# Loads and stores of H, of the filter blocks, of the bias table and of the heads' scales issued from GpSimd's queue, in a two-layer attention and long-convolution encoder on one Trainium2 core

## The chip, the core and the metric

The kernel runs on one core of one Trainium2 chip. The metric is the device time of one execution in microseconds (us), launch to end. Before the change three runs gave 963.81, 966.33 and 965.6 us, with a median of 965.6 us. The engines are called as the profile does: PE (matmul), PEld (its weight loads), DVE (vector), ACT (scalar), POOL (GpSimd), SP (the engine that here only issues transfers). "SPq" is SP's own sequence of transfer issues, "POOLq" that of POOL.

## The reference, cut to what matters

```python
DEPTH, SEQ, D_MODEL = 2, 512, 1024
for l in range(DEPTH):
    h = rms_norm(x, pre_norm[l], NORM_EPS)
    q, k, v, z_a, u_h, z_h, g_a, g_h = jnp.split(h @ w_in[l], splits, axis=-1)
    o = diff_attention(q, k, v, lam, rel_bias)             # 4 heads, two softmaxes each, table of relative biases
    o = rms_norm(o, subln[l], SUBLN_EPS) * (1.0 - lam_init)
    y_a = o * jax.nn.silu(z_a)
    hv, hx1, hx2 = jnp.split(short_conv3(u_h, conv_w[l], conv_b[l]), 3, axis=-1)
    filt = hyena_filters(S, ..., flt_w_out[l], flt_deltas[l])   # rfft of long filters, made from small weights
    z = fft_long_conv(hv, filt[:, 0], flt_bias[l, 0]) * hx1
    z = fft_long_conv(z, filt[:, 1], flt_bias[l, 1]) * hx2
    m = jax.nn.sigmoid(g_a) * (y_a @ w_pa[l]) + jax.nn.sigmoid(g_h) * (z * jax.nn.silu(z_h)) @ w_ph[l]
    x = x + rms_norm(m @ w_out[l], post_norm[l], NORM_EPS)
```

## The kernel before, in words

All work is in float32, and every product is made of three matmuls on operands split in two: `split` lets ACT cast the source to `hi` (line 207) and DVE form `lo = source - hi` (line 208). Weights come in blocks of 256 KB: `weights` loads a block into `wraw` (three buffers), and splits it into `whi` and `wlo`. The buffer of a block is free when DVE has made its `wlo`.

The stages of a layer follow one another, but are mixed: the norm of four row tiles of 128 (`ss`, `rinm` on DVE at line 224, `rin` on POOL at line 226, the scaling `s` on DVE at line 519, transposes on PE at line 530, `hT`), then the input projection; four attention heads (`head_rows`, `head_norm`, `head_scale`); the long convolutions, done as matrix products with blocks of a Fourier matrix (`fh`, `fl`, constants that POOL fetches at the start); the output projections; and the border to the next layer (`routm` and `rout`, then again `rinm` and `rin`).

The filters of the convolutions don't depend on x. They are computed in eight blocks for the layers' two orders and two channel halves, in gaps of the other stages: `filter_load` fetches `flt_deltas`, `flt_w_out` (in two pieces) and `flt_bias`; `filter_group` makes a piece of the spectrum and stores it to a tensor in DRAM, `H` (`H_408` to `H_411`). The convolutions read it back into `ld` (two buffers) and `hb` (one). A head loads its bias rows from the table `tab`, which the kernel has written to DRAM, into `ld`. `head_norm` makes the scale of a head's rows on POOL (`ro`, line 689); `head_scale` transposes it on PE (line 696), writes 2 KB to DRAM (`rd`), reads it back spread over all partitions (`b`, three buffers), and DVE multiplies with it (line 703).

No order is written out by hand beyond this. A list scheduler with costs and priorities of its own (`high_priority`, `ahead`) places every instruction in its engine's sequence, and each engine then works through its sequence in order: an issue that waits for a buffer holds all that stands behind it on the same engine. Before the change SP issues every transfer (`load` at line 181, `store` at line 184) but four, which POOL issues: `fh` and `fl` (line 252), `a3d` (line 361) and `a` from `a3d` (line 407).

Of the kernel before, what the change touches and what calls it, by code (L numbers as in the profile page):

```python
# [17 lines left out]
P = 128  # L18
# [116 lines left out]
def ahead(n):  # L135

    def wrap(f):
        def g(self, *args):
            with self.tc.high_priority(offset=n):
                return f(self, *args)  # L140
        return g
    return wrap
# [3 lines left out]
class Net:  # L146
# [35 lines left out]

    def store(self, out, src):
        self.nc.sync.dma_start(out=out, in_=src)

    def mm3(self, out, pairs):

        n = 3 * len(pairs)
        i = 0
        for lh, ll, rh, rl in pairs:  # L190
            for l, r in ((lh, rh), (lh, rl), (ll, rh)):
                self.nc.tensor.matmul(out, lhsT=l, rhs=r, start=(i == 0), stop=(i == n - 1))  # L192
                i += 1
# [209 lines left out]
    def filter_load(self, l, o, hc, st):  # L403
        nc, a = self.nc, self.a
        if l and o == hc == 0:
            self.a3 = self.cst.tile([P, 512], F32R, name="a3", tag="a3")
            nc.gpsimd.dma_start(out=self.a3, in_=self.a3_next)
        raw = self.t("b", a=2)
        dl = self.t("yh", a=4)[:, 0:2] if st["where"] == "convs" else self.t("u", a=2)
        self.load(dl, a["flt_deltas"][l].rearrange("(d o h c) -> d o h c", d=2, o=2, h=2)[:, o, hc].partition_broadcast(P))  # L410
        src = a["flt_w_out"][l].rearrange("k (d o h c) -> k d o h c", d=2, o=2, h=2)[:, :, o, hc]
        for j in range(2):
            self.load(raw[j * 64:(j + 1) * 64], src)
        nc.scalar.activation(out=dl, in_=dl, func=AF.Abs)
        hi, lo = (self.t("u" if st["where"] == "heads" else "za", F32R, 2) for _ in range(2))
        self.split(hi, lo, raw)
        st.update(dl=dl, hi=hi, lo=lo, T=[self.two(st) for _ in range(2)])
        br = st["bias"] = self.sm.tile([P, 256], F32, name="fbias", tag="fbias", bufs=1)
        self.load(br[0:1, :], a["flt_bias"][l, o:o + 1, hc * 256:hc * 256 + 256])

    @ahead(-20)
    def filter_taps(self, l, t, st):
# [49 lines left out]
    def filter_group(self, l, o, hc, im, ft, st):  # L472

        nc = self.nc
        ps = self.ps("po", 2)
        yh, yl = st["in", im, ft ^ im]
        f, c = "EO"[ft], "CS"[im]
        even = [(c + "E" + f, yh[:, 0], yl[:, 0])]
        if im == 0:
            zh, zl = st["in", 0, 0]  # L480
            even.append((("FA", "FB")[ft], zh[:, 0], zl[:, 0]))
        self.dft_sum(ps[:, 0], even)
        self.dft_sum(ps[:, 1], [(c + "O" + f, yh[:, 1], yl[:, 1])])

        s = 1.0 * 2 / NF if ft else self.nt[:, NT_RE + im:NT_RE + im + 1]
        odd, hs = self.t("b", a=2)[:, 0], self.t("b", a=2)
        nc.scalar.activation(out=odd, in_=ps[:, 1], func=AF.Copy, scale=s)
        for j, op in ((0, ALU.add), (1, ALU.subtract)):  # L490
            nc.vector.scalar_tensor_tensor(out=hs[:, j], in0=ps[:, 0], scalar=s, in1=odd, op0=ALU.mult, op1=op)
        H = self.H[l][o][:, hc]
        if ft:
            self.store(H[:, 6 + 2 * im:8 + 2 * im], hs)
        elif im:
            self.store(H[:, 4:6], hs)
            d = self.t("b", a=2)
            for j in range(2):
                nc.scalar.activation(out=d[0:1, j], in_=ps[0:1, 1], func=AF.Copy, scale=(1.0 - 2 * j) / NF)
            self.store(H[0:1, 1:4:2], d[0:1])  # L500
        else:
            self.store(H[:, 0:4:2], hs)
            self.store(H[:, 1:4:2], hs)


    def new_hT(self):
# [115 lines left out]
    @ahead(20)  # L622
    def head_rows(self, l, h, i, st):


        nc = self.nc
        if i == 0:
            st["B"] = self.t("ld")
            t = self.tab[h:h + 1, :]
            self.load(st["B"][:, :896], bass.AP(tensor=t.tensor, offset=t.offset + 1, ap=[[1, P], [1, 896]]))  # L630
            st["s"] = self.small(8, "s")
        tsl = slice(i * P, (i + 1) * P)
        s0, s1 = (st["s"][:, 4 * c + i:4 * c + i + 1] for c in range(2))
        p = []
        for c in range(2):
            ps = self.ps("pq")
            for n in range(2):
                nc.tensor.matmul(ps, lhsT=st["q"][c][:, tsl], rhs=st["k"][c][n], start=(n == 0), stop=(n == 1))  # L638
            lg = self.t("a")
            m = self.small(1, f"m{c}")  # L640
            nc.vector.tensor_tensor_reduce(out=lg, in0=ps, in1=st["B"][:, 384 - i * P:896 - i * P], scale=1.0, scalar=3e38,  # L641
                                           op0=ALU.add, op1=ALU.min, accum_out=m)
            nc.scalar.activation(out=lg, in_=lg, func=AF.Exp, scale=-1.0, bias=m, accum_out=(s0, s1)[c])  # L643
            p.append(lg)
        r = self.small(1, "r")
        nc.vector.reciprocal(out=r, in_=s1)
        n1 = self.small(1, "n1")
        nc.vector.scalar_tensor_tensor(out=n1, in0=r, scalar=self.nlam[:, l:l + 1], in1=s0, op0=ALU.mult, op1=ALU.mult)
        nc.vector.scalar_tensor_tensor(out=p[0], in0=p[1], scalar=n1, in1=p[0], op0=ALU.mult, op1=ALU.add)
        st[i] = p[0]  # L650
# [41 lines left out]
    def head_scale(self, l, h, st):  # L692
        nc = self.nc
        u, pss, r = st["u"], st["o"], st["r"]

        nc.tensor.transpose(out=pss[0:4, 128:256], in_=r, identity=self.ident)
        rows = self.t("b")
        nc.scalar.copy(out=rows[0:4, :P], in_=pss[0:4, 128:256])
        rd = self.dram.tile([4, P], F32, name=f"rd{l}{h}", tag=f"rd{l}{h}")
        self.store(rd, rows[0:4, :P])  # L700
        rb = self.t("b")
        self.load(rb, rd.rearrange("i q -> (i q)").partition_broadcast(P))
        nc.vector.tensor_tensor(out=tiles(u), in0=tiles(u), in1=tiles(rb)[:, :, ::-1], op=ALU.mult)
        hi, lo = self.t("ya", F32R), self.t("ya", F32R)
        self.split(hi, lo, u)
        self.ya.append((hi, lo))
# [87 lines left out]
    @ahead(30)  # L794
    def conv_group(self, l, o, hc, st, ft):

        nc = self.nc
        H = self.H[l][o][:, hc]
        first, b = self.t("ld", a=4), None
        if ft:  # L800
            self.load(first, H[:, 6:10])
            A, B = first[:, 0:2], first[:, 2:4]
        else:
            B = self.t("hb", a=2)
            self.load(first, H[:, 0:4])
            self.load(B, H[:, 4:6])
        yh, yl = st["Y"]
        f = "EO"[ft]
        U = [self.ps("pq", 2) for _ in range(2)]
        for j, t in enumerate("EO"):  # L810
            re = [("C" + t + f, yh[:, j], yl[:, j])]
            im = [("S" + t + f, yh[:, 2 + j], yl[:, 2 + j])]
            if t == f == "E":
                re.append(("XA", yh[:, 2], yl[:, 2]))
                im.append(("XB", yh[:, 0], yl[:, 0]))
            self.dft_sum(U[j][:, 0], re)
            self.dft_sum(U[j][:, 1], im)
        odd = self.t("a", a=2)
        nc.scalar.copy(out=odd, in_=U[1])

        X, W = self.t("cx", a=4), self.t("cx", a=4)
        for s, op in ((0, ALU.add), (1, ALU.subtract)):
            nc.vector.tensor_tensor(out=X[:, 2 * s:2 * s + 2], in0=U[0], in1=odd, op=op)  # L823
        four = lambda t: t.rearrange("p (s c) x -> p s c x", s=2)
        both = lambda t: t.rearrange("p (s c) x -> p s c x", c=1).broadcast_to([P, 2, 2, 256])
        nc.vector.tensor_tensor(out=four(W), in0=four(X), in1=both(B), op=ALU.mult)  # L826
        nc.vector.tensor_tensor(out=four(X), in0=four(X), in1=both(A) if ft else four(first), op=ALU.mult)  # L827
        nc.vector.tensor_tensor(out=X[:, 0:4:2], in0=X[:, 0:4:2], in1=W[:, 1:4:2], op=ALU.subtract)
        nc.vector.tensor_tensor(out=X[:, 1:4:2], in0=X[:, 1:4:2], in1=W[:, 0:4:2], op=ALU.add)

        for s, op in ((0, ALU.add), (1, ALU.subtract)):
            nc.vector.tensor_tensor(out=W[:, 2 * s:2 * s + 2], in0=X[:, 0:2], in1=X[:, 2:4], op=op)  # L832
        st["Q", f] = self.t("s1", F32R, 4), self.t("s1", F32R, 4)
        self.split(*st["Q", f], W)
# [264 lines left out]
```

## Time and profile before

| what | value |
|---|---|
| runs | 963.81, 966.33, 965.6 us; median 965.6 |
| profiled execution | 964.57 us, of which the span is 962.8 |
| PE busy | 920.7 us (96%) |
| DVE busy | 734.0 us (76%) |
| ACT busy | 467.6 us (49%) |
| POOL busy | 42.0 us (4%) |
| mean granted TensorE clock | 0.993 |

The span runs from the first to the last instruction of the profiled execution; 1.77 us of its time lie around it. An engine's busy time doesn't count the issuing of transfers; that is seen in the timelines of SPq and POOLq, where a row's first number is the start of an issue and its second its duration. In a timeline, the bracket at the end of a row gives the idle time ahead of it on its engine and what ended it.

### The profile page before, as it was taken

What the parts mean: (1) busy time and instruction counts of PE and PEld (TensorE: products, weight loads), DVE (VectorE), ACT (ScalarE), POOL (GpSimd) and SP (SyncE); (2) the same over time, 40 slices, a digit from 0 to 9 for tenths busy, and PEclk for the clock granted to TensorE, in tenths of its full rate; (3) what the DMA queues carried; (4) which work ended last, traced back from release to release, by engine and by line L of the source; (5) the groups of instructions that cost most, each with busy time, mean ns of one, the idle gap of its engine ahead of it and who ended that gap; (6) DMA issues with size and microseconds to landing.
All of it is one profiled execution on the core that took longest, in us unless ns stands there. A gap on an engine that the chain in (4) does not pass through costs nothing. (4 is left out here: it accounts for less than half of the span.)

```text
span 962.8 us, 14325 instructions
## 1 busy us (share of the span) xinstructions
PE 920.7 (96%) x5139; PEld 793.0 (82%) x5139; DVE 734.0 (76%) x1439; ACT 467.6 (49%) x927; POOL 42.0 (4%) x58
## 2 busy tenths in 40 slices
PE   3999999999899989999999999999999998999997
PEld 3878988887788878878889888888888887888897
DVE  4889789789889978888657486686798898854533
ACT  4586576555344334555435465564444433333431
POOL 2000100002000000000001000000000000000000
PEclk9999999999999999999999999999999999999999
DMA  7341541533534443345645323333343644233422
GB/s 243 108 135 53 151 131 51 166 104 87 148 115 128 123 114 117 102 129 153 208 133 165 92 85 96 88 89 117 91 121 88 197 121 125 82 90 98 139 71 88
DMA packets 147692, 114.18 MB, mean 119 GB/s; under 512 B 7106, under 2 KB 134752, under 8 KB 147621
## 3 DMA queue, kind: packets, MB, share of 16 engines
q1 hardware_dynamic: 147045, 111.31, 39.1%
q0 software_dynamic: 576, 1.97, 0.6%
q8 instruction: 40, 0.66, 0.3%
q14 instruction: 31, 0.25, 0.1%
HBM read 98.26 MB, written 14.99 MB: 118 GB/s over the span
## 5 line engine op out<-in xcount | busy, mean ns | idle before, releaser
L192 PE MATMUL pd<-hT,whi 128*128 128x512 f32 x1408 | 455.1, 396 | 3.1 <-ACT a L887 2.6
L192 PEld LDWEIGHTS pd<-hT,whi 128*128 128x128 f32 x1408 | 261.0, 188 | 55.3 <-ACT a L887 3.3
L192 PE MATMUL pd<-hT,wlo 128*128 128x512 f32 x704 | 278.2, 395 | 3.7 <-DVE wlo L208 3.6
L207 ACT CAST whi<-wraw 128x512 fp32r<-128x512 f32 x228 | 140.9, 619 | 222.1 <-PE pd L192 112.8
L208 DVE TENSOR_TENSOR wlo<-wraw,whi 128x512 fp32r<-128x512 f32 x228 | 154.6, 686 | 67.4 <-ACT whi L207 66.5
L192 PEld LDWEIGHTS pd<-hT,wlo 128*128 128x128 f32 x704 | 132.5, 188 | 30.9 <-DVE wlo L208 4.5
L643 ACT ACTIVATE a<-a,m 128x512 f32<-128x512 f32 x64 | 46.1, 721 | 21.8 <-DVE m L641 20.7
L638 PE MATMUL pq<-s,s 128*128 128x512 f32 x128 | 47.1, 402 | 1.4 <-DVE m L641 1.3
L641 DVE CUSTOM_DVE_ANT_0 a<-pq,ld 128x512 f32<-128x512 f32 x64 | 43.1, 685 | 3.8 <-PE pq L638 3.1
L192 PE MATMUL pd<-whi,hT 128*128 128x256 f32 x192 | 38.8, 298 | 5.6 <-ACT whi L207 5.6
L722 DVE SCALAR_TENSOR_TENSOR u<-pd,vec,u 128x256 f32<-128x256 f32 (+2 forms) x80 | 39.3, 530 | 3.6 <-ACT u L720 3.3
L192 PE MATMUL pd<-ya,whi 128*128 128x512 f32 x128 | 41.7, 393 | 0.0
L192 PE MATMUL pd<-yh,whi 128*128 128x512 f32 x128 | 39.5, 389 | 0.0
L192 PEld LDWEIGHTS pd<-whi,hT 128*128 128x128 f32 x192 | 32.2, 202 | 6.3 <-ACT whi L207 6.2
L204 PE MATMUL po<-s,fh 128*128 128x256 f32 x160 | 31.4, 296 | 4.6 <-ACT s L207 2.0
L207 ACT CAST s<-cx 128x1024 fp32r<-128x1024 f32 x24 | 25.2, 1050 | 21.9 <-DVE cx L832 19.0
L204 PE MATMUL pq<-s,fh 128*128 128x256 f32 x160 | 34.7, 291 | 0.0
L204 PEld LDWEIGHTS po<-s,fh 128*128 128x128 f32 x160 | 26.0, 199 | 7.3 <-ACT s L207 2.8
L935 DVE TENSOR_TENSOR yh<-pd,s 128x256 f32<-128x256 f32 x32 | 13.3, 421 | 24.0 <-ACT a L933 23.3
L208 DVE TENSOR_TENSOR s<-cx,s 128x1024 fp32r<-128x1024 f32 x24 | 29.3, 1222 | 0.8 <-ACT s L207 0.8
L638 PEld LDWEIGHTS pq<-s,s 128*128 128x128 f32 x128 | 23.2, 188 | 7.7 <-DVE m L641 2.5
L192 PE MATMUL po<-s,yh 128*128 128x256 f32 x192 | 28.8, 285 | 0.5 <-ACT s L207 0.4
(221 smaller groups left out, 1661.5 us busy)
## 6 DMA issues: line engine op xcount, KB each, us to landing
wraw<-in_w_in SPq DMA_DIRECT2D x192, 256.0 KB
H<-b SPq DMA_DIRECT2D x40, 256.0 KB
ld<-H SPq DMA_DIRECT2D x16, 512.0 KB
wraw<-in_w_out SPq DMA_DIRECT2D x32, 256.0 KB
wraw<-in_w_pa SPq DMA_DIRECT2D x16, 256.0 KB
wraw<-in_w_ph SPq DMA_DIRECT2D x16, 256.0 KB
ld<-tab SPq DMA_DIRECT2D x8, 448.0 KB
yh<-in_x SPq DMA_DIRECT2D x4, 512.0 KB
```

What stands on the lines that cost most here:

```text
L192: self.nc.tensor.matmul(out, lhsT=l, rhs=r, start=(i == 0), stop=(i == n - 1))
L204: self.nc.tensor.matmul(out, lhsT=b, rhs=y, start=(i == 0), stop=(i == len(ops) - 1))
L207: self.nc.scalar.copy(out=hi, in_=src)
L208: self.nc.vector.tensor_tensor(out=lo, in0=src, in1=hi.bitcast(F32), op=ALU.subtract)
L638: nc.tensor.matmul(ps, lhsT=st["q"][c][:, tsl], rhs=st["k"][c][n], start=(n == 0), stop=(n == 1))
L641: nc.vector.tensor_tensor_reduce(out=lg, in0=ps, in1=st["B"][:, 384 - i * P:896 - i * P], scale=1.0, scalar=3e38, op0=ALU.add, op1=ALU.min ...
L643: nc.scalar.activation(out=lg, in_=lg, func=AF.Exp, scale=-1.0, bias=m, accum_out=(s0, s1)[c])
L722: nc.vector.scalar_tensor_tensor(out=o, in0=src, scalar=w[j], in1=o, op0=ALU.mult, op1=ALU.add)
L935: nc.vector.tensor_tensor(out=st["o"][tt][:, cs], in0=ps, in1=g, op=ALU.mult)
```

## The change

A new helper `side` issues a transfer from POOL's queue. 128 transfers, until then issued by SP, go through it: for each of the eight filter blocks one load of `flt_deltas`, two of `flt_w_out` and one of `flt_bias` (32); 48 stores to H (40 of 256 KB, 8 of 2 KB); 8 loads of 448 KB from `tab`; 8 stores of 2 KB to `rd` and 8 loads of 256 KB from it; 24 loads of H (16 of 512 KB into `ld`, 8 of 256 KB into `hb`). The weights, x, the gains, the constants, and the stores of x and of the output stay with SP.

```diff
+    def side(self, out, src):
+
+        self.nc.gpsimd.dma_start(out=out, in_=src)
+
@@ filter_load
-        self.load(dl, a["flt_deltas"][l].rearrange("(d o h c) -> d o h c", d=2, o=2, h=2)[:, o, hc].partition_broadcast(P))
+        self.side(dl, a["flt_deltas"][l].rearrange("(d o h c) -> d o h c", d=2, o=2, h=2)[:, o, hc].partition_broadcast(P))
...
-            self.load(raw[j * 64:(j + 1) * 64], src)
+            self.side(raw[j * 64:(j + 1) * 64], src)
...
-        self.load(br[0:1, :], a["flt_bias"][l, o:o + 1, hc * 256:hc * 256 + 256])
+        self.side(br[0:1, :], a["flt_bias"][l, o:o + 1, hc * 256:hc * 256 + 256])
@@ filter_group
-            self.store(H[:, 6 + 2 * im:8 + 2 * im], hs)
+            self.side(H[:, 6 + 2 * im:8 + 2 * im], hs)
...
@@ head_rows
-            self.load(st["B"][:, :896], bass.AP(tensor=t.tensor, offset=t.offset + 1, ap=[[1, P], [1, 896]]))
+            self.side(st["B"][:, :896], bass.AP(tensor=t.tensor, offset=t.offset + 1, ap=[[1, P], [1, 896]]))
@@ head_scale
-        self.store(rd, rows[0:4, :P])
+        self.side(rd, rows[0:4, :P])
         rb = self.t("b")
-        self.load(rb, rd.rearrange("i q -> (i q)").partition_broadcast(P))
+        self.side(rb, rd.rearrange("i q -> (i q)").partition_broadcast(P))
...
-            self.load(first, H[:, 0:4])
-            self.load(B, H[:, 4:6])
+            self.side(first, H[:, 0:4])
+            self.side(B, H[:, 4:6])
```

The other stores and loads of H are edited in the same way. The scheduler plans anew with these issues on POOL, so the sequences of the other engines change at places too; of PE's 5,104 instructions the first 146 rows of its sequence stand as before, then some groups are exchanged. Line numbers of the changed kernel are 4 higher behind the helper, and the moved transfers have the helper's line, 188.

On DVE the start of the program reads so before the change. `s_141` to `s_302` are the four row tiles of x on their way to `hT`, `wlo` the lower halves of the first weight blocks.

```order
L224 TENSOR_SCALAR rinm<-ss 128x1
L519 SCALAR_TENSOR_TENSOR s_141<-yh,rin,s_127 128x512 x2
L224 TENSOR_SCALAR rinm<-ss 128x1
L519 SCALAR_TENSOR_TENSOR s_192<-yh,rin,s_127 128x512 x2
L208 TENSOR_TENSOR hT<-pt,hT 128x2x128
L224 TENSOR_SCALAR rinm<-ss 128x1 x2
L519 SCALAR_TENSOR_TENSOR s_248<-yh,rin,s_127 128x512
L208 TENSOR_TENSOR wlo<-wraw,whi 128x512 x3
L208 TENSOR_TENSOR hT<-pt,hT 128x2x128 x2
L519 SCALAR_TENSOR_TENSOR s_248<-yh,rin,s_127 128x512
L208 TENSOR_TENSOR hT<-pt,hT 128x2x128 x2
L208 TENSOR_TENSOR wlo<-wraw,whi 128x512
```

The same piece of DVE's sequence after the change:

```order
L228 TENSOR_SCALAR rinm<-ss 128x1 x2
L523 SCALAR_TENSOR_TENSOR s_141<-yh,rin,s_127 128x512 x2
L523 SCALAR_TENSOR_TENSOR s_192<-yh,rin,s_127 128x512 x2
L228 TENSOR_SCALAR rinm<-ss 128x1
L523 SCALAR_TENSOR_TENSOR s_248<-yh,rin,s_127 128x512
L212 TENSOR_TENSOR wlo<-wraw,whi 128x512
L212 TENSOR_TENSOR hT<-pt,hT 128x2x128
L212 TENSOR_TENSOR wlo<-wraw,whi 128x512 x2
L212 TENSOR_TENSOR hT<-pt,hT 128x2x128 x2
...
L212 TENSOR_TENSOR wlo<-wraw,whi 128x512
L212 TENSOR_TENSOR hT<-pt,hT 128x2x128 x2
L228 TENSOR_SCALAR rinm<-ss 128x1
```

The `rinm` of the second row tile now stands ahead of `s_141`, and that of the fourth behind the fourth `wlo`. POOL's `rin` of a tile needs that tile's `rinm`, and `fh` and `fl` stand behind all four `rin` in POOL's sequence in both kernels.

On POOL the border of the layers and the first two heads of layer 1 read so before (`s_5936` to `s_6824` are parts of the heads' keys that are set to zero):

```order
L226 TENSOR_TENSOR rout<-routm,nhalf 128x1
L226 TENSOR_TENSOR rin<-rinm,nhalf 128x1
L611 MEMSET s_5936 64x512
L611 MEMSET s_5941 64x512
...
L689 TENSOR_TENSOR ro<-rom,nhalf 128x4
L611 MEMSET s_6819 64x512
L611 MEMSET s_6824 64x512
L689 TENSOR_TENSOR ro<-rom,nhalf 128x4 x3
```

And after the change, the same stretch of POOL from the last `rout` of the border to the second `ro` of layer 1 (the rows left out are a `rin`, MEMSETs and two more `ld<-tab`):

```order
L188 DMA ld<-tab 128x896
L230 TENSOR_TENSOR rout<-routm,nhalf 128x1
...
L188 DMA ld<-tab 128x896
L693 TENSOR_TENSOR ro<-rom,nhalf 128x4
L188 DMA rd_6492<-b 4x128
L188 DMA b<-rd_6492 128x512
L615 MEMSET s_6819 64x512
L188 DMA yh<-in_flt_deltas 128x2x256
L615 MEMSET s_6824 64x512
L188 DMA ld<-H_410 128x1024
L693 TENSOR_TENSOR ro<-rom,nhalf 128x4
```

A load into `ld` now stands on POOL directly ahead of the fourth `rout` of the border, and ahead of the first and the second `ro` of layer 1. Each of these loads waits, as it did on SP, for its buffer.

## Rows read from the trace of the kernel before

**Rows 1.** The page: span, and busy time of each engine.
```profile
span 962.8 us, 14325 instructions
PE 920.7 (96%) x5139; PEld 793.0 (82%) x5139; DVE 734.0 (76%) x1439; ACT 467.6 (49%) x927; POOL 42.0 (4%) x58
```
**Rows 2.** Stretches: start:end, length, then busy time by engine, clock, DMA.
```profile
0.00:24.10 24.10, 9.42 (x44) 8.51 (x45) 10.44 (x24) 10.07 (x21) 5.11 (x14) 0.95 0.77 243
24.10:938.70 914.60, 893.68 (x4951) 767.18 (x4950) 714.05 (x1392) 454.25 (x893) 34.66 (x40) 1.00 0.40 116
```
**Rows 3.** Timeline of PE, start: what ends its first and its fourth gap.
```profile
8.09 1.94 PE L530 MATMUL pt<-ident,s 128*128 128x128 f32 x8 [8.09 <-DVE s L519]
...
21.88 0.80 PE L192 MATMUL pd<-whi,hT 128*128 128x256 f32 x2 [2.20 <-ACT whi L207]
```
**Rows 4.** Waits of SP's queue: total us, times, longest us.
```profile
SPq L181 <- DVE wlo L208: 407.6, 173, 12.0
SPq L184 <- DVE b L491: 56.5, 28, 7.7
```
**Rows 5.** Waits of ACT and DVE for transfers, in the same columns.
```profile
ACT whi L207 <- DMA wraw<-in_w_in: 59.4, 31, 7.0
...
DVE b L703 <- DMA b<-rd: 5.4, 4, 2.8
```
**Rows 6.** Timeline of SP's queue where it issues a filter's loads.
```profile
402.34 0.89 SPq L184 DMA_DIRECT2D H<-b  x2
...
404.90 1.25 SPq L181 DMA_DIRECT2D b<-in_flt_w_out  x2
```
**Rows 7.** ACT and PE behind those loads.
```profile
411.02 0.62 ACT L207 CAST za<-b 128x512 fp32r<-128x512 f32 x1 [1.18 <-DMA b<-in_flt_w_out]
411.69 0.38 PE L428 MATMUL pq<-za,a 128*128 128x256 f32 x1 [1.28 <-ACT za L207]
```
**Rows 8.** The start: the fourth weight block on SP and ACT, DVE, POOL's issues.
```profile
14.98 0.40 SPq L181 DMA_DIRECT2D wraw<-in_w_in  x1
21.21 0.62 ACT L207 CAST whi<-wraw 128x512 fp32r<-128x512 f32 x1 [3.07 <-DMA wraw<-in_w_in]
10.24 0.15 DVE L224 TENSOR_SCALAR rinm<-ss 128x1 f32<-128x1 f32 x1 [1.63 <-ACT s L515]
14.27 1.89 DVE L208 TENSOR_TENSOR wlo<-wraw,whi 128x512 fp32r<-128x512 f32 x3
14.03 0.72 POOL L252 DMA_DIRECT2D fh<-in_c_fh  x1
14.75 0.54 POOL L252 DMA_DIRECT2D fl<-in_c_fl  x1
```
**Rows 9.** Page, transfers: a 256 KB load that POOL issues, us to landing.
```profile
a3d<-u POOLq DMA_DIRECT2D x1, 256.0 KB, 3.2
```
**Rows 10.** Timeline of POOL, and of DVE beside its row.
```profile
223.11 4.59 POOL L755 COPY u<-u 128x1 f32<-128x1 f32 x1 [5.94 <-DVE u L747]
226.97 0.68 DVE L829 TENSOR_TENSOR cx<-cx 128x512 f32<-128x512 f32 x1
```
**Rows 11.** SP and POOL at the border of the layers.
```profile
517.60 0.33 SPq L181 DMA_DIRECT2D ld<-tab  x1
519.33 0.86 POOL L226 TENSOR_TENSOR rout<-routm,nhalf 128x1 f32<-128x1 f32 x1 [3.26 <-DVE routm L224]
```
**Rows 12.** Second head of layer 1: SP, POOL and PE.
```profile
630.58 0.34 SPq L181 DMA_DIRECT2D ld<-H  x1
630.77 1.32 POOL L689 TENSOR_TENSOR ro<-rom,nhalf 128x4 f32<-128x4 f32 x1 [35.58 <-DVE rom L687]
632.15 0.27 PE L696 MATMUL po<-ident,ro 128*4 128x128 f32 x1
```
**Rows 13.** A load of H, and the first instruction that reads it.
```profile
298.03 0.34 SPq L181 DMA_DIRECT2D hb<-H  x1
324.66 1.22 DVE L826 TENSOR_TENSOR cx<-cx,hb 128x1024 f32<-128x1024 f32 x1
```

More of the change, by code (lines that the diff above doesn't have):

```diff
@@ L493, in filter_group @@
         if ft:
-            self.store(H[:, 6 + 2 * im:8 + 2 * im], hs)
+            self.side(H[:, 6 + 2 * im:8 + 2 * im], hs)
         elif im:
-            self.store(H[:, 4:6], hs)
+            self.side(H[:, 4:6], hs)
             d = self.t("b", a=2)
@@ L499, in filter_group @@
                 nc.scalar.activation(out=d[0:1, j], in_=ps[0:1, 1], func=AF.Copy, scale=(1.0 - 2 * j) / NF)
-            self.store(H[0:1, 1:4:2], d[0:1])
+            self.side(H[0:1, 1:4:2], d[0:1])
         else:
-            self.store(H[:, 0:4:2], hs)
-            self.store(H[:, 1:4:2], hs)
+            self.side(H[:, 0:4:2], hs)
+            self.side(H[:, 1:4:2], hs)
     def new_hT(self):
@@ L800, in conv_group @@
         if ft:
-            self.load(first, H[:, 6:10])
+            self.side(first, H[:, 6:10])
             A, B = first[:, 0:2], first[:, 2:4]
```

## The prediction

> **What bounds the kernel now.** The page comes first: PE is busy for 920.7 of 962.8 us, DVE for 734.0, POOL for 42.0 [rows 1]. PE is the bound nearly everywhere, so whatever the change does must show in PE's 42.1 us of idle time: 962.8 less 920.7. The stretches say where that lies. In the first 24.1 us PE works 9.42, so 14.68 are idle there; from 24.1 to 938.7 it works 893.68 of 914.60, so 20.92 are idle in nineteen twentieths of the program [rows 2]. The rest, 6.5 us, is the end, behind the last transfer that the change moves. A change that leaves PE's work as it is can at most win a part of 14.7 and 20.9 us, and loses wherever it makes PE wait anew.
>
> PE's timeline of the start shows what ends its gaps there: the first scaled row tile at 8.09 us, and at 21.88, after 2.20 us without work, a weight block that ACT had to wait for [rows 3]. The third view is SP's waits, since the change is about what stands behind what on SP. SP waits 407.6 us in 173 waits for a `wlo`, that is for a weight block's own buffer; the stores of H hold it for 56.5 us in 28 waits [rows 4]. The second number looks like the prize. But a weight load can only be issued when its buffer is free, and the queue's long waits are for just that. A store that blocks SP costs a weight load something only when a buffer comes free meanwhile, and where that happens, in the stage at 402 to 408 us, SP issues two stores and two filter loads of 1.25 us before it comes to the next weight block [rows 6]; there the delay is one to two microseconds of a transfer's lead.
>
> **The change part by part.** The sum is made against the profiled execution, 964.57 us, which is 1.03 below the median of the runs (965.6).
>
> *Issues that leave SP.* 128 issues of 0.3 to 0.6 us each are gone from SP; 0.34 for a `ld` load, 0.45 for a store of H, 0.62 for a piece of `flt_w_out` [rows 6, 11, 12]. SP is idle or waiting for buffers most of the time, so the issues themselves give nothing; what they held back does. Two waits in the views could shrink. ACT waits 59.4 us in 31 waits for a weight block's landing [rows 5], but ACT is busy only 467.6 of 962.8 us [rows 1], and PE's 20.92 us between 24.1 and 938.7 are an upper bound to all of it. I take 0.3 us as an estimate, with 0 to 5 as its bounds: 5 would be a quarter of those 20.92.
>
> *Issues that go to POOL.* The rows of POOL's own issues are 0.72 (`fh`) and 0.54 (`fl`) [rows 8]. 128 times 0.6 is 77 us more on POOL, 119 of 963 in all, so POOL does not become the bound. A transfer that POOL issued landed 3.2 us after its issue (256 KB) [rows 9]. What counts is what stands behind an issue in POOL's order.
>
> *ro behind a load.* In layer 1 a load of H stands ahead of the second head's `ro`. SP issued it at 630.58; `ro` ran from 630.77 for 1.32 us, to 632.09, and PE's transpose followed at 632.15 [rows 12]. With 0.6 us for the issue, `ro` starts at 631.18, 0.41 later, and PE waits about 0.4. The other heads have an issue ahead that lies earlier or PE comes later. Term: +0.4, bounds 0 to 1.3 (an issue as long as `ro` itself).
>
> *rd and the heads' scales.* DVE waits 5.4 us in 4 of the 8 cases for the scale to come back through DRAM [rows 5]. Two issues of about 0.6 instead of 0.3 lie in that chain: 0.6 more in each of the 4, 2.4 on DVE. DVE is busy 76% of the time, and only a part reaches PE: I take 0.5, bounds 0 and 2.4.
>
> *Filter loads.* At 402 to 406 us PE's work hangs on `flt_w_out`: ACT casts it at 411.02 after a wait of 1.18, PE waited 1.28 for that [rows 6, 7]. On POOL the two stores, the deltas, one store and the two pieces take 6 x 0.6 from 402.34, to 405.94, against 406.15 on SP: equal. With a landing as that of `a3d`, 3.2 [rows 9], they are there at 409.2, and the 1.28 would go; with issues of 0.72 and a landing as on SP (411.0 less 406.15, so 4.8) it grows by 0.5. I take 0 between -1.28 and +0.5.
>
> *Loads of H* are early: one issued at 298.03 is read at 324.66 [rows 13]. Twenty-six microseconds hide any landing shown here; the cover would be gone only if the issue came more than 20 us late. The four `rout` of the border: the load from `tab` ahead of the fourth was issued at 517.60, `rout` at 519.33 [rows 11]; 0.6 us of issue is over at 518.2, with 1.1 to spare. The MEMSETs behind moved issues write keys of a later head than the one in work. All three at 0.
>
> *The start, which the scheduler orders anew.* The fourth weight block was issued at 14.98 and cast at 21.21, so it took 6.2 us, while `fh` and `fl`, 1,408 KB together, had been issued at 14.03 and 14.75 ahead of it [rows 8]. In the new order the fourth `rinm` stands behind the fourth `wlo`, so `rin` of the fourth tile, and with it `fh` and `fl`, come after that block has landed. Without them, and with a landing between that of `a3d` (3.2) and one half as long again (4.8, an estimate), it is there at 18.2 to 19.8, and cast 0.62 later. PE has other work until 21.88 - 2.20 = 19.68 [rows 3], so it could go on between 19.7 and 20.4. I take 20.1, a gain of 1.8. Against it stands the other exchange: `s_141` now waits for the second `rinm`, which ran at 10.24, so with 0.15 for it and 0.7 for half of `s_141` PE's first transposes come at 11.1 instead of 8.09. They filled 1.94 us of a stretch in which PE then idled until the first weights, so 3 us of delay don't reach the end as such; the first `wlo` moves from 14.27 to some 14.7, and so does the fourth block's buffer. Term: -1.8 + 0.4 = -1.4, bounds -2.2 (the whole gap) and +0.5.
>
> **The sum**: -0.3 + 0.4 + 0.5 + 0 - 1.4 = -0.8 us, against 964.57: 963.8 for an execution such as the profiled one, and 964.8 against the median, which is the number given. Bounds together: -5.0 + 0 + 0 - 1.3 - 2.2 = -8.5, and 0 + 1.3 + 2.4 + 0.5 + 0.5 = +4.7.
>
> **A rule weighed against the trace.** What could make an issue on POOL long? POOL's COPY of 128x1 at 223.11 took 4.59 us, and ended at 227.70, when a run of DVE instructions with two operands in SBUF ended at 227.65 [rows 10]; it moves one element per partition. So POOL can be shut out by DVE. Yet `fl` was issued at 14.75 in 0.54 us while DVE ran three `wlo` of this same kind, from 14.27 for 1.89 us [rows 8]. The issue was not shut out.
>
> The Trainium skill, page "SBUF — State Buffer", section "SBUF: two separate sides", warns against just this change: descriptors of a transfer that GpSimd issues are written by GpSimd, which DVE can lock out of a shared port, so that a transfer of some 620 ns took about 3,100; it advises to issue from SP or ACT. Its section "Who interferes with whom" narrows it: a `tensor_tensor` with two SBUF inputs holds off GpSimd's reads, not its writes. The trace agrees with both on the COPY and with the narrower reading on `fl`. By the first reading, with 3.1 us for an issue (the page's figure), the three places of the second rival below would be late by 1.4, 2.9 and an estimated 2, and the time 971; by the second reading it is the sum above.
>
> **The rivals.**
>
> *Faster, by separate queues.* Weights no longer wait behind stores of H, in SP's order or in the transfers themselves, and a good part of the 20.92 us closes. For it: the 59.4 us of ACT's waits and the 56.5 us of SP's [rows 4, 5]. Against it: PE idles little behind them. A quarter of 20.92 plus the start: -5.2 - 1.4, so 965.6 - 6.6 = 959.0 at best, 961 as its middle. Chance 0.27.
>
> *Slower, by shut-out issues.* If an issue on POOL lasts as long as the COPY, 4.59 us, wherever DVE is dense, three places decide. The `rout` at 519.33 would begin at 517.60 + 4.59 = 522.19, 2.9 late; `ro` at 630.77 at 635.17, 4.4 late [rows 11, 12]; the six issues at 402.34 would end up to 24 us later, of which the other work in PE's order hides most, so 3 as an estimate from the 1.28 lost there now [rows 7]. That is +10.3, so 975 at worst; with issues of half that length, 2.3, the three are 0.6, 2.1 and 1.5, so 969. It decides from an issue of about 1.7 us on, where `rout` begins to be late (517.60 to 519.33). Chance 0.20.
>
> *No gain at the start, and the other small terms at their upper bounds.* The new order costs what it gives: 965.6 + 0.4 + 0.5 + 0.5, so 967 and up to 970.3 (+4.7). Part of this is within the bound of no change; chance of being beyond it 0.08.
>
> **How the numbers follow.** The three runs lie 0.26% apart; I take 0.3%, 2.9 us, as what can be told from no change: 962.7 to 968.5. The forecast, 964.8, lies inside, chance 0.45 with what the third rival leaves inside. Faster 0.27 and slower 0.20 + 0.08 follow. The range for 8 in 10 takes in the faster rival's middle with some to spare and the slower one with issues of half length: 958.5 to 970.5. The likeliest case's own range is 962 to 967.
>
> **What would show it.** Right: moved issues of 0.5 to 0.75 us on POOL also under dense DVE; PE's gap at 21.88 gone and PE working again at about 20; `fh` and `fl` issued after 20 us; the second `ro` of layer 1 about 0.4 later beside its neighbours; PE's idle time between 24 and 938 us within 2 of 20.9. Wrong: issues of over 1.7 us on POOL, `rout` or `ro` waiting for POOL and not for DVE, PE idle on `ro` or `hT`; or, the other way, ACT's 59.4 us of waiting for weights halved and PE's idle time in the middle below 16.

## The result, and the profile after

The changed kernel takes 1015.86 us (median of 4 runs, 1013.93 to 1016.33) against 965.38 before (a fourth run, 965.16, has joined the three): 1.0511 times as long, with a 95% interval of 1.0482 to 1.0539, some 50 us slower. The forecast was no change, with 958.5 to 970.5 as its range.

The page of the changed kernel, with the rows that answer to [rows 1], the queue that takes POOL's transfers (packets, MB, share of 16 DMA engines' span) and the busy time of the moved stores of H (in the last row the numbers behind the bar are the sum and the mean in ns, then POOL's idle time ahead of them):

```profile
span 1014.6 us, 14377 instructions
PE 942.6 (93%) x5139; PEld 807.4 (80%) x5139; DVE 735.1 (72%) x1439; ACT 466.4 (46%) x927; POOL 113.4 (11%) x186
PEclk9899999999799989988999999999999998999999
q0 software_dynamic: 10176, 32.95, 11.0%
L188 POOL DMA_DIRECT2D H<-b x48 | 29.6, 618 | 137.3 <-DVE b L495 135.9
```

The span grew by 51.8 us. PE does the same 5,139 matmuls in 942.6 us instead of 920.7, and is idle for 72.0 instead of 42.1 (1014.6 less 942.6). So 29.9 us are new idle time, and 21.9 are matmuls that ran longer: PEclk, nines throughout before, now has eights and a seven. DVE and ACT are no busier. POOL's busy time does count its issues, other than the section on the profile before has it: of its 186 rows 128 are the moved transfers. They last what was expected of them, 0.62 us for a store of H. Before, the queue `q0` had 576 packets and 1.97 MB: the moved transfers are not only issued by another engine, they also come by another queue than SP's (`q1 hardware_dynamic` on the page).

PE's timeline shows the new gaps, each with what ended it:

```profile
258.79 0.79 PE L196 MATMUL pd<-hT,wlo 128*128 128x512 f32 x1 [3.99 <-DVE wlo L212]
364.95 0.58 PE L208 MATMUL po<-s,fh 128*128 128x256 f32 x1 [3.19 <-ACT s L211]
440.86 0.79 PE L432 MATMUL pq<-za,a 128*128 128x256 f32 x2 [4.66 <-ACT za L211]
474.80 0.58 PE L432 MATMUL pq<-za,a 128*128 128x256 f32 x1 [3.27 <-ACT za L211]
711.75 0.42 PE L196 MATMUL po<-s,yh 128*128 128x256 f32 x1 [3.41 <-ACT s L211]
856.37 0.58 PE L208 MATMUL po<-s,fh 128*128 128x256 f32 x1 [4.95 <-ACT s L211]
```

The stretches around three of them (length, busy time of PE, PEld, DVE, ACT and POOL, then the granted clock, DMA share, GB/s):

```profile
252.00:283.00 31.00, 23.64 (x100) 19.12 (x99) 20.21 (x36) 11.45 (x20) 3.75 (x6) 0.83 0.46 133
358.00:384.00 26.00, 21.34 (x102) 17.75 (x101) 17.59 (x32) 8.26 (x14) 1.26 (x2) 0.87 0.38 112
836.00:862.00 26.00, 20.77 (x102) 17.53 (x100) 18.50 (x26) 6.10 (x10) 2.19 (x4) 0.87 0.44 122
```

Behind such a gap PE runs for some microseconds at the lower of its two clock levels (1.2 instead of 2.4 GHz): in the stretch from 252 the mean granted clock is 0.83, where before it was 0.97 in the same 31 us and 1.00 on the mean of the whole middle [rows 2]. So a gap costs more than its own length, and this is all of the 21.9 us: PE's busy time multiplied by the mean granted clock is 914.3 before (920.7 x 0.993) and 914.3 after (942.6 x 0.970). The hundred PE instructions from 251.9 to 283.3 us begin 15.4 us later than before and end 21.5 later, 6.1 more; the gaps among them, 3.99 and another of 3.00, are 7.0 us against 4.6 in the same place before.

Three more waits. SP now waits for little but the weights' own buffers, ACT waits no less than before for the weights' landing, and DVE waits longer for the scales (before: [rows 4, 5]):

```profile
SPq L181 <- DVE wlo L212: 660.6, 193, 24.7
...
ACT whi L211 <- DMA wraw<-in_w_in: 66.4, 27, 7.5
...
DVE b L707 <- DMA b<-rd: 18.0, 8, 4.7
```

SP's queue was freed, then, and the weights gained nothing by it: ACT waits 66.4 us for them instead of 59.4.

### The profile page after: what moved, and what is told of

The parts are those of the page before. It is cut to its first block, busy times and chain, and to the rows that moved or that the text cites. A ratio compares the mean times of both kernels' runs of the same rounds, so it can differ in the third digit from the quotient of the medians.

```text
span 1014.6 us, 14377 instructions
## 1 busy us (share of the span) xinstructions
PE 942.6 (93%) x5139; PEld 807.4 (80%) x5139; DVE 735.1 (72%) x1439; ACT 466.4 (46%) x927; POOL 113.4 (11%) x186
## 5 line engine op out<-in xcount | busy, mean ns | idle before, releaser
L196 PE MATMUL pd<-hT,whi 128*128 128x512 f32 x1408 | 463.6, 402 | 4.8 <-ACT a L891 2.9
L196 PEld LDWEIGHTS pd<-hT,whi 128*128 128x128 f32 x1408 | 267.2, 193 | 58.7 <-ACT a L891 4.0
L196 PE MATMUL pd<-hT,wlo 128*128 128x512 f32 x704 | 282.8, 402 | 5.3 <-DVE wlo L212 5.2
L196 PEld LDWEIGHTS pd<-hT,wlo 128*128 128x128 f32 x704 | 135.4, 192 | 34.2 <-DVE wlo L212 6.8
L188 POOL DMA_DIRECT2D H<-b x48 | 29.6, 618 | 137.3 <-DVE b L495 135.9
L208 PE MATMUL po<-s,fh 128*128 128x256 f32 x160 | 34.2, 314 | 11.5 <-ACT s L211 8.1
L208 PEld LDWEIGHTS po<-s,fh 128*128 128x128 f32 x160 | 28.3, 217 | 14.1 <-ACT s L211 9.0
L432 PE MATMUL pq<-za,a 128*128 128x256 f32 x96 | 24.2, 308 | 7.9 <-ACT za L211 7.9
```

What stands on the lines that cost most here:

```text
L188: self.nc.gpsimd.dma_start(out=out, in_=src)
L208: self.nc.tensor.matmul(out, lhsT=b, rhs=y, start=(i == 0), stop=(i == len(ops) - 1))
L432: nc.tensor.matmul(ps[:, d], lhsT=self.a3[:, t * P:(t + 1) * P], rhs=w[:, d], start=(n == 0), stop=(n == 1))
```

## The experiments

**One family of transfers at a time.** In each of four kernels a part of the edits stands and the rest is as before; the second moves nothing but a kilobyte per filter block. Every ratio below is to the kernel before, run beside it: 964.18 us for e1 to e4, 964.73 for e5 to e8, 964.01 for e9 to e12. One or two lines of each edit:

```diff
 e1: the three loads of H in conv_group
-            self.load(first, H[:, 6:10])
+            self.side(first, H[:, 6:10])
...
 e2: only the loads of flt_bias
-        self.load(br[0:1, :], a["flt_bias"][l, o:o + 1, hc * 256:hc * 256 + 256])
+        self.side(br[0:1, :], a["flt_bias"][l, o:o + 1, hc * 256:hc * 256 + 256])
...
 e3: the five stores in filter_group
-            self.store(H[:, 4:6], hs)
+            self.side(H[:, 4:6], hs)
...
 e4: the loads from tab in head_rows, the store and load of rd in head_scale
-        self.store(rd, rows[0:4, :P])
+        self.side(rd, rows[0:4, :P])
```

> Of the 128 moved transfers only the 24 loads of H (16 of 512 KB, 8 of 256 KB) are issued from POOL. PE's sequence is that of the kernel before, ACT's and DVE's differ in a few places. Theory A (a load on POOL's queue is carried at the same time as the weight blocks of SP's queue and makes them land later; ACT and DVE then wait in order, PE idles, and its clock falls after the idle time): the gaps of the changed kernel at 364.95 (3.19), 856.37 (4.95) and part of that at 258.79 (3.99) come back, with slower clock behind them, so 8 to 18 us slower than before. Theory B (the scheduler's new order makes the time): no order, no cost, so within 2 us of before.

> Only the 8 loads of flt_bias (1 KB each) are issued from POOL: practically no data moves, but the scheduler plans anew, with 220 lines of PE's sequence, 70 of ACT's and 118 of DVE's different from before (614, 222 and 226 in the changed kernel). Theory A: within 4 us of before. Theory B: a good part of the 50 us, 10 to 25 us slower.

> Only the 48 stores to H are issued from POOL. Theory A: weights issued while two or three stores are in flight land late, and the next filter piece waits for its buffer: 5 to 18 us slower. Theory B: 400 lines of PE's sequence differ from before, so 10 to 25 us slower. The run itself does not tell A from B; its size goes into the sum by parts.

> Only the 8 loads from the bias table and the 8 stores and 8 loads of the heads' scales are issued from POOL. Theory A, for the scales: the 2 KB store to DRAM is no longer held by weights in its queue, and no load of H stands in POOL's queue ahead of it here, so DVE's wait for the scale stays near 5 to 9 us (18.0 in the changed kernel, 5.4 before), and with the eight table loads (448 KB each) the time is 2 to 8 us above before. Theory B: 150 lines of PE's sequence differ, 5 to 12 us slower.

Measured: e1 1.0135 (1.0114 to 1.0156), 13.0 us slower; e2 1.0038 (1.0020 to 1.0057), 4.0; e3 1.0054 (1.0034 to 1.0075), 5.5; e4 1.0109 (1.0081 to 1.0137), 10.8. In e2 220 lines of PE's sequence moved and little came of it (theory B had asked for 10 to 25), so a different order is not dear in itself; it depends on which places are exchanged. e3 lies within A's bounds and below B's, e4 above A's 2 to 8 and within B's; in e4 DVE's wait for the scales, expected at 5 to 9 us, is 17.4, though on POOL's queue there are only the table's loads beside them. By its expectation e1 spoke for theory A, since PE's sequence is that of before. Its trace says otherwise. ACT's timeline in e1, where a convolution's cast `s` and the next weights meet:

```profile
341.04 0.62 ACT L211 CAST whi<-wraw 128x512 fp32r<-128x512 f32 x1 [6.17 <-DMA wraw<-in_w_in]
344.51 0.62 ACT L211 CAST whi<-wraw 128x512 fp32r<-128x512 f32 x1 [2.85 <-DMA wraw<-in_w_pa]
345.03 1.04 ACT L211 CAST s<-cx 128x1024 fp32r<-128x1024 f32 x1
```

and the same place in the kernel before:

```profile
337.87 0.62 ACT L207 CAST whi<-wraw 128x512 fp32r<-128x512 f32 x1 [6.10 <-DMA wraw<-in_w_in]
339.54 1.04 ACT L207 CAST s<-cx 128x1024 fp32r<-128x1024 f32 x1 [1.05 <-DVE cx L832]
341.19 0.62 ACT L207 CAST whi<-wraw 128x512 fp32r<-128x512 f32 x1 [0.60 <-DMA wraw<-in_w_pa]
```

The reader is to see two things. The weight block `w_pa` does not land much later: SP issued it at 339.67 in e1 and at 336.57 before, so it took 4.84 and 4.62 us. But ACT's order is another. Before, `s` is cast while the block is on its way; in e1 the block's cast stands ahead of `s`, waits 2.85 us, and `s`, for which PE is waiting, comes out 5.5 us after where it did (345.03 against 339.54), while the program as a whole is only some 3 us later there. The eight differing lines of ACT's sequence in e1 are four such exchanges. Set beside the same instruction before, PE falls back at three of them, by 3.1, 3.2 and 3.9 us (near 252, 346 and 816 us); together these are 10.2 of the 11.7 us by which the profiled execution is longer. The text of the expectation had set "no order, no cost" against PE's sequence only; ACT's eight lines were the thing to look at. Hence a second series, which parts the queue from the order.

**Queue and order apart.** The three compute engines can be held to a list: each instruction of PE, ACT and DVE gets an edge that lets it be issued only behind the one that precedes it in the list. No semaphore is added by that, and the list is taken from another build:

```diff
+def follow(tc):
+    traced = {i.name: i for i in tc.nc.cur_bb.bb.instructions}
+    info = mybir.DependencyInfo(mybir.DependencyClass.NoSync, mybir.DependencyReason.DATA)
...
+        for first, then in zip(names, names[1:]):
+            tc.add_manual_dep(traced[then], first, info, reason="order")
...
         Net(ctx, tc, aps).run()
+        follow(tc)
```

Four kernels: the changed kernel with the lists of before (e5), the kernel before with the lists of the changed one (e6), and the same two for the loads of H alone (e7, e8). The lists do not bind SP and POOL, but little moves there: against the kernel before, 4 of SP's 313 issues in e5 and 16 of 441 in e6 come at another place, in e7 and e8 none.

> All 128 transfers on POOL's queue as in the changed kernel, but PE, ACT and DVE are held to the sequences of the kernel before, instruction by instruction. Theory A (the two queues disturb each other): most of the 50 us stays, 990 to 1016. Theory B (ACT and DVE are placed by a plan in which the weights land early once the other transfers have left SP's queue; on the chip they land no earlier, and what stands behind them waits): most of it goes, 962 to 978, the rest being the scales' longer way through DRAM and the filter loads.

> The kernel before, every transfer issued from SP as there, but PE, ACT and DVE are held to the sequences of the changed kernel. Theory A: near before, 962 to 975. Theory B: near the changed kernel or above it, 990 to 1030, since the early places for the weights' casts are kept and SP's queue is no faster.

> The 24 loads of H on POOL's queue as in the run with them alone (13 us slower), with PE, ACT and DVE held to the sequences of the kernel before: four casts of weights stand behind a cast of the convolution again instead of ahead of it. Theory A: the 13 us stay, 974 to 980. Theory B: within 3 us of before.

> No transfer moved; PE, ACT and DVE in the sequences of the run with the H loads alone, that is four casts on ACT and two subtractions on DVE one place or a few earlier. Theory A: within 3 us of before. Theory B: 8 to 16 us slower than before.

Measured, as ratios to the kernel before with their intervals:

| | order of before | new order |
|---|---|---|
| all 128, from SP | 1 | e6: 1.0263 (1.0214 to 1.0312) |
| all 128, from POOL | e5: 1.0298 (1.0251 to 1.0346) | the change: 1.0511 (1.0482 to 1.0539) |
| loads of H, from SP | 1 | e8: 1.0141 (1.0099 to 1.0182) |
| loads of H, from POOL | e7: 1.0023 (0.9999 to 1.0047) | e1: 1.0135 (1.0114 to 1.0156) |

For the loads of H it is the order: four exchanged casts (with two subtractions on DVE that moved along), and every transfer where it was, cost 11.9 us, and the queue with the old order 2.4 us, at the edge of what can be told (the interval takes in 1). In e8 the picture of e1 is there again, with the load of H on SP's queue:

```profile
346.93 0.62 ACT L207 CAST whi<-wraw 128x512 fp32r<-128x512 f32 x1 [2.76 <-DMA wraw<-in_w_pa]
347.46 1.04 ACT L207 CAST s<-cx 128x1024 fp32r<-128x1024 f32 x1
...
348.55 0.58 PE L204 MATMUL po<-s,fh 128*128 128x256 f32 x1 [3.18 <-ACT s L207]
```

For the whole change neither theory stands alone. Order by itself is 23 us, the queue by itself 27, each within some 5, and together they make about the 50. Both A and B had each claimed most of it, and both were wrong in that: e6's 988.01 lies in neither's range, and e5's 991.72, though just inside A's, has little more than half of the loss. Nor is the queue's half what A says: in e5 the weights land no later (ACT waits 58.3 us for them, first row below, 59.4 before). Of the 23 us of order, about 10 are PE's steps at the same three casts as in e1 (3.4, 3.2 and 3.3 in e6); about 8 lie where `flt_w_out` is cast, between 400 and 450 us, and about 5 at the border of the layers. Which exchanges make these was not tested.

**What in the queue costs 27 us.** In e5 the new gaps are at flt_w_out and at the scales. ACT's wait for weights, ACT and PE at flt_w_out, and the stretch behind the first gap:

```profile
ACT whi L211 <- DMA wraw<-in_w_in: 58.3, 29, 7.1
...
424.55 0.62 ACT L211 CAST za<-b 128x512 fp32r<-128x512 f32 x1 [1.80 <-DMA b<-in_flt_w_out]
425.22 0.58 PE L432 MATMUL pq<-za,a 128*128 128x256 f32 x1 [3.83 <-ACT za L211]
425.00:450.00 25.00, 24.78 (x115) 21.02 (x116) 21.76 (x45) 12.82 (x26) 4.18 (x7) 0.88 0.31 96
```

and POOL's queue at a scale's round trip:

```profile
656.50 0.58 POOL L188 DMA_DIRECT2D rd<-b  x1 [0.92 <-ACT b L702]
661.13 0.58 POOL L188 DMA_DIRECT2D b<-rd  x1 [4.05 <-DMA rd<-b]
```

The first gap answers to [rows 7], where PE waited 1.28 for the same cast: it is 3.83 now, and 0.88 in the granted clock for the 25 us behind it. The long landings are those that hold PE: of the 16 pieces of `flt_w_out` the four at its gaps of 3.83 and 4.35 (at 460.19), issued with three or four transfers of POOL's queue still in flight, took 6.0 to 7.5 us; the other twelve, with two at most, 2.8 to 4.5. In the second view the load issues 4.63 us after the 2 KB store that it waits for; before, from SP, it was 633.47 to 635.16, 1.69. Three kernels send these parts back to SP (`self.side` to `self.load` or `self.store` in those lines), with the order of before:

> As the run with all transfers on POOL's queue in the old order (27 us slower), but the 32 filter loads go back to SP. There PE's wait for flt_w_out (gaps of 3.83 at 425.22 and 4.35 at 460.19, with the slower clock behind them) makes steps of 5.3 and 6.5 us. Theory A1 (flt_w_out comes late because it stands in POOL's queue behind three stores of H): those two steps go, 10 to 13 us less, 977 to 983. Theory A2 (the sheer number of transfers at once makes all land late): less than 4 us come back.

> As the run with all transfers on POOL's queue in the old order, but the stores and loads of the heads' scales (16 transfers) go back to SP. From the issue of the 2 KB store to that of the load that waits for it, 2.1 us on the mean before, 3.7 there; DVE waits 22.2 us for the 8 scales instead of 5.4, and the steps at the first and the seventh head are about 5 and 5.9 us. Theory A1 (the round trip through DRAM is longer on POOL's queue): 8 to 12 us less, 979 to 984. Theory A2 (the waits are made by the other transfers in flight, wherever the scales go): under 3 us less.

> Both go back to SP; on POOL's queue stay H's stores and loads and the bias table's loads, in the old order. By theory A1 the two parts add up: 2 to 8 us slower than before, 967 to 973.

Measured: e9 981.13 us (1.0196, 1.0165 to 1.0227), e10 983.38 (1.0210, 1.0182 to 1.0238), e11 971.39 (1.0092, 1.0064 to 1.0119), beside 991.72 for e5. So the filter loads from POOL cost 10.6 us (e5 less e9) or 12.0 (e10 less e11), the scales 8.3 (e5 less e10) or 9.7 (e9 less e11), and 7.4 are left for H's stores and loads and the bias table (e11 less 964.01, the kernel before). Each difference is known to some 4 to 6 us only, by the intervals; within that the parts add up. In the profiled executions of e9 and e11, 11.0 and 9.7 us lie behind PE's last matmul, instead of 6.6 before, where no moved transfer stands; what makes these 4.5 and 3.2 us the record doesn't show. With the scales back on SP DVE waits 7.8 us for them instead of 22.2, and from the store's issue to that of the load it is 2.4 instead of 3.7.

**The order at the start.** The forecast's one gain was the fourth weight block without `fh` and `fl` ahead of it. The last kernel tries that alone: the kernel before, with its sequences held, in which only `fh` and `fl` come later on POOL:

```diff
-            self.load_dft()
             self.vectors()
+            seen = self.const([P, 1], "seen")
+            self.tc.keep_in_program_order(self.nc.gpsimd.tensor_copy(out=seen, in_=self.vec[:, 0:1]))
+            self.load_dft()
```

> The kernel before, its PE, ACT and DVE sequences unchanged and no transfer moved to another queue; only fh and fl are issued later on POOL, behind a copy of one column that waits for DVE's vec (about 27 us) instead of at 14.03 and 14.75 us. If the fourth weight block lands late because of them (6.2 us from issue to cast), PE's gap of 2.20 at 21.88 closes: 1.5 to 2.2 us faster than before. If it is late for another reason, no change.

Measured: 959.19 us, ratio 0.9953 (0.9933 to 0.9974), 4.5 us by the ratio, where 1.5 to 2.2 had been expected. It is faster than both kernels. The sequences of PE, ACT, DVE and SP are those of before. ACT's cast of that block, and the first 24.1 us:

```profile
17.40 0.62 ACT L207 CAST whi<-wraw 128x512 fp32r<-128x512 f32 x1
...
0.00:24.10 24.10, 12.25 (x78) 11.41 (x79) 13.84 (x34) 12.63 (x28) 2.86 (x10) 1.00 0.65 199
```

The block was issued at 14.35 and is cast at 17.40, without a wait in the row; before it was 14.98 and 21.21 [rows 8]. The gap of 2.20 is gone, PE works 12.25 us of the stretch instead of 9.42, and its mean granted clock there is 1.00 instead of 0.95 [rows 2]. What the expectation had left out is the clock again: before, PE ran at a granted clock of 0.50 from 21.88 to 25.20, behind the gap. And 0.6 us of the profiled execution's gain is there at its first matmul (7.47 instead of 8.09), before either kernel issues `fh`.

## Why the prediction was wrong

*What bounds the kernel* was read rightly as far as the gain goes: SP's long waits were for the weights' own buffers, and freeing SP gave nothing. (From 402 to 406 us SP issues three stores and three filter loads, not two of each; nothing hangs on that.) The Trainium skill, page "DMA: Bandwidth & Descriptors", section "Issuing engines are not separate DMA queues", says that transfers started by different engines run on the same DMA engines, so that a second issuer saves only issue time. The traces agree: the block at 339.67 in e1 took 4.84 us, that of before 4.62.

*Issues that go to POOL*: 0.6 each was forecast, and POOL at 119 us in all; 0.51 to 0.78 and 113.4 were measured. The second rival, issues shut out by DVE, did not happen, so the side it stood for was right and its mechanism wrong. The trace agrees there with the narrower reading of the Trainium skill, page "SBUF — State Buffer", section "Who interferes with whom".

*The step that failed first* is "The start, which the scheduler orders anew": the new order was priced in that one place, and front and prediction alike spoke of the rest as some groups that are exchanged. It is 23 us by itself (e6), of which e8 shows 11.9 to come of four casts. The scheduler plans with its own idea of when a load has landed. With H's loads gone from SP's sequence it let ACT cast a weight block ahead of the convolution's `s`; on the chip the block came no earlier, ACT waited in its order, and PE waited for `s`. That the plan counts on an earlier landing is inferred from where it puts the casts; that the place of the casts makes the time is shown, by e8 and e7.

*The filter loads* were put at 0, between -1.28 and +0.5. They cost 10.6 to 12.0 us. Even the time of issue was near (416.35 us for the first piece in e5, 2.8 behind the first store, against 2.6 before), but the landing taken for it, 3.2, was that of a transfer that was alone in POOL's queue; here the two pieces came behind stores and deltas in the same queue, and the second, issued at 416.96, was cast at 424.55 as soon as it was there, 7.6 us after. And PE's waits, 3.83 and 4.35, each brought a spell at the lower clock: the steps they made in PE's progress are 5.3 and 6.5 us.

*The heads' scales* were put at 0.5, at most 2.4. They cost 8.3 to 9.7. The reckoning had 0.6 more for two issues; measured from the store's issue to that of the load that waits for it are 3.7 us on the mean of eight in e5, against 2.1 before. The store's landing grew, more than its issue (0.56 instead of 0.27). Most of this comes with POOL's queue itself and not with the other moved transfers: with the table's loads alone beside the scales (e4) it is 3.3, and DVE waits 17.4 us in all; with the scales on SP and all the others on POOL (e10) it is 2.4, and DVE waits 7.8.

*ro behind a load*, +0.4 and at most 1.3, was a small term as forecast: PE's idle time on `ro` is 1.4 in the whole changed kernel, in two waits of 0.8 at most. *Loads of H* as data are hidden (e7).

*The start* was forecast at -1.4. The mechanism holds and its size is larger when it is alone (e12). In the changed kernel the gain is there (the 101st matmul starts at 29.50, 2.67 earlier than before) and is lost again at once: DVE waits 5.00 for one of the loads for the lambdas, until 34.07, and an `hT` behind it holds PE at 34.88 for 1.99. `fh` and `fl`, now issued at 22.03, run beside those loads; that they make them late was not tested.

*A cost that the sum had no term for* is the clock. The prediction began with it that whatever the change does must show in PE's 42.1 us of idle time, and every bound was made of that; 21.9 of the 51.8 us are PE's longer busy time, at the lower clock, mostly behind gaps of 2 to 5 us.

## What to carry to other kernels

Where a scheduler orders the engines, the queue of a transfer is an input to its plan: compare every in-order engine's sequence, not only that of the engine that is the bound, and look for an instruction that waits for a transfer and was put ahead of one that the bound engine needs. Holding the sequences to a recorded list parts the effect of a new queue from that of a new order in two runs. A queue's cost can lie in the moved transfers themselves, though each issue is short: look at what waits for them, and at what is in flight ahead of them. And new gaps on PE of 2 to 5 us are dearer than their length: here 51.8 us came from 29.9 of new idle time.

## What the runs showed of the hardware that was not expected

A 2 KB store to DRAM and the load that waits for it took 3.3 to 3.7 us from issue to issue on POOL's queue (means of eight in four kernels), against 2.1 before and 2.4 in e10 and e11 on SP's, while POOL's issues themselves were short. A piece of `flt_w_out` on POOL's queue took 2.8 to 7.5 us to land, 6.0 and more where three or four transfers of that queue were in flight ahead of it. And two large loads that nothing needed until 103 us (fh's first use) cost 4.5 us in all, by a weight block that was cast 6.23 us after its issue beside them and 3.05 without them: the gap of 2.20 is a half of it, and PE's 101st matmul starts at 27.57 instead of 32.17 (0.6 of this from the first matmul on), with the granted clock of the start at 1.00 instead of 0.95.
